# Modulation vectors of a two-layer backbone: direct products on TensorE replaced by wider sums on VectorE

## The chip, the core and the metric

The kernel runs on one core of a Trainium2 chip. The metric is the device time of one execution in microseconds, as the median of several; smaller is better. The engines are PE (TensorE, the matrix engine), DVE (VectorE), ACT (ScalarE), POOL (GpSimd) and SP, whose queue issues nearly all loads.

## The reference, cut to what matters

Two layers run over 256 latent and 256 context tokens of width 1024. Each layer is a feed-forward stage, a token mixer and a second feed-forward stage, and each of the three is wrapped in normalisations whose shift, scale and gate vectors come from the conditioning vectors `c` and `c_ctx` through one large matrix `w_ada` (1024 x 9216 for each layer, 36 MB in float32):

```python
def rms_norm(x, g):
    return x * rsqrt(mean(x * x, axis=-1) + EPS) * g
def ada_pre(x, mod, j, g):
    return rms_norm(x, g) * (1.0 + mod[..., 3 * j + 1, :]) + mod[..., 3 * j, :]
def ada_post(x, y, mod, j, g, w):
    return x + w * mod[..., 3 * j + 2, :] * rms_norm(y, g)
def macaron_ffn(x, mod, j, g_pre, g_post, w1, w3, w2):
    h = ada_pre(x, mod, j, g_pre)
    y = (silu(h @ w1) * (h @ w3)) @ w2
    return ada_post(x, y, mod, j, g_post, 0.5)
...
    mod_x = (silu(c) @ w_ada[l] + b_ada[l]).reshape(B, 1, 9, D)
    mod_c = (silu(c_ctx) @ w_ada[l] + b_ada[l]).reshape(1, 1, 9, D)
    # feed-forward (j=0), token mix (j=1), feed-forward (j=2), for latent and context tokens
```

## The kernel before, in words

The stages follow each other as F0_0 (first feed-forward of layer 0), mix0, F1_0, F0_1, mix1, F1_1. Activations lie transposed, 128 channels by tokens; the context tokens are columns 0 to 255, the latent ones 256 to 511. Each float32 weight tile is split into a high part (a cast on ACT, line 240, tile wh) and a low part (a subtraction on DVE, line 241, tile wl), and each product is made of three matrix products, lines 257 to 259 ("main products" below).

A feed-forward stage has 11 blocks gi, each with 256 columns of W1 and 256 of W3 (96 main products of 128x512). Behind each block stand the gates, lines 595 to 599: silu on ACT, a multiply on DVE (596), a cast, and a subtraction on DVE (599). Then come four groups dg of the down projection with W2; in dg 3 the two token streams are done one after the other by `part`. Weights are loaded by the SP queue into three raw tiles and split into four pairs wh, wl.

The modulation vectors are cut into units of 256 columns of `w_ada`, 36 a layer. The first eight of layer 0 are made in the setup. The other 64 are "fillers", and two ways are in use:

- Summed on DVE (`mod_acc`), 48 units: two in each of the blocks gi 0 to 7 of F0_0, F1_0 and F0_1, loaded by `preload` at the block before. A unit is 16 DVE operations of 128x256 (line 306 for the first of each column of `sc`, line 308 for the seven accumulations), which leave per-partition sums. Every fourth unit closes a batch: PE sums the partitions by products with ones (line 317), ACT copies the result (320), PE transposes it (four products, line 326), DVE adds the bias into `mods` (328).
- Direct products on PE (`mod_mm`), 16 units: eight are loaded at the end of F0_0 (the 8 in `FIN`) and eight at the end of mix0 (`MIXB`), and `flush`, called in `passes`, makes them at the start of mix0 and of F1_0. A unit is eight products with `sc` as the weights (line 277), an ACT copy (279), two small products (284) and a DVE add (285).

`passes` makes the first products of a stage, stream by stream. For the second stream the input still has to be normalised: `Post.steps` sums squares and cross terms (PE, lines 474 to 497; the row sums of line 488 come first), then runs a chain of small DVE operations (`rsqrt_cols`, lines 358 to 367) for the output norm of the stage that ends, a broadcast of its result over rows on PE (line 372), a second such chain for the input norm of the next stage, and a second broadcast. The multiplies of line 529 need the first broadcast, the scaled inputs of lines 387 (DVE), 395 (ACT) and 396 (DVE) the second. Line 348 makes gate vectors of the stage to come from `mods`.

PE, SP, DVE and ACT run in an order that a scheduler fixes when the program is built. It has no table by hand; the order follows from what each engine has to do and from `issue_after` for single instructions, so it can change where work is added or taken away.

Of the kernel before, what the change touches and what calls it, by code (L numbers as in the profile page):

```python
# [20 lines left out]
KD = 8  # L21
# [23 lines left out]
ACC, BX, MX = 3, 2, 3  # L45
FIN = ((16, 8), (16, 0), (16, 0), (0, 0))
MIXB = ((0, 8), (0, 0))
PU = 2

# [27 lines left out]
def body(tc, I, out, dbg=None):  # L77
    nc = tc.nc
    with tc.tile_pool(name="cst", bufs=1) as cst, \
# [188 lines left out]
        def settle():  # L268
            while late:
                late.pop(0)()  # L270
# [22 lines left out]
        batch = []  # L293

        def mod_acc(l, u, raw):
            if len(batch) % 2 == 0:
                pair = slab()
            else:
                pair = batch[-1][2]
            batch.append((l, u, pair))  # L300
            for s in range(2):
                t = pair[:, (len(batch) - 1) % 2, 256 * s:256 * s + 256]
                for k in range(KD):
                    w, c = raw[k // 4][:, k % 4, :], sc[:, k, s:s + 1]
                    if k == 0:
                        V.tensor_scalar(t, w, c, None, op0=ALU.mult)
                    else:
                        V.scalar_tensor_tensor(t, w, c, t, op0=ALU.mult, op1=ALU.add)  # L308
            if len(batch) < 4:
                return  # L310
            items = batch[:]
            batch.clear()

            def sums():
                bank = mx()
                for j in range(4):
                    mm(bank[32 * j:32 * j + 32, :], one1.to_broadcast([128, 32]), items[j][2][:, j % 2, :], start=True, stop=True,
                       tile_position=(0, 32 * j))
                sb = tmp()
                S.copy(sb, bank)  # L320

                def rest():
                    p2 = mx((128, 2, 2, 128))
                    for s in range(2):
                        for i in range(2):
                            nc.tensor.transpose(p2[:, s, i, :], sb[:, 256 * s + 128 * i:256 * s + 128 * i + 128], ident)
                    for j, (l, u, _) in enumerate(items):
                        V.tensor_tensor(mods[l][:, 2 * u:2 * u + 2, :], p2[:, :, :, 32 * j].rearrange("p s i -> p i s"),
                                        par[f"b{l}"][:, 2 * u:2 * u + 2, None].to_broadcast([128, 2, 2]), op=ALU.add)

                late.append(rest)

            late.append(sums)
# [218 lines left out]

        def preload(n):
            for _ in range(n):
                if fillers:
                    m = fillers.pop(0)
                    ahead.append((*m, mod_load(*m, True)))

        def flush(n):
            settle()  # L560
            for _ in range(n):
                if ahead:
                    mod_mm(*ahead.pop(0), S.copy)

# [8 lines left out]
        def passes(accs, h, sts, hook=None):  # L573
            n = len(ahead)
            for s_, (lo, hi, _) in enumerate(sts):
                flush(-(-n // len(sts)))
                for i in range(KD):
                    for j, (ps, w, c0) in enumerate(accs):
                        if hook:
                            hook(i, j)  # L580
                        end = mm3(ps[:, lo:hi], w[i:i + 1], c0, h[i:i + 1], lo, hi, i == 0, i == KD - 1)
                    if s_ == 0 and pend and i in (1, 5):
                        pend[0].step(end)
                drain(end)

        def ffn(l, f, h, post, streams, pre, first=(None, None)):
# [3 lines left out]
            units, hook = first  # L590
            nxt = []

            def gate(p1, p3):
# [8 lines left out]
            for gi in range(KF // 2):  # L602
# [36 lines left out]
                if gi + 1 == KF // 2:  # L639
                    nxt.append(unit(W2[0:1024, 0:256], 8))  # L640
                for _ in range(len(late)):
                    late.pop(0)()
                while ahead:
                    mod_acc(*ahead.pop(0))
                if gi < 9:
                    preload(min(PU, FIN[2 * l + f][0] - PU * gi))
            st = [slab(), slab()]
# [7 lines left out]
            for dg in range(4):  # L655
# [11 lines left out]
                if dg < 3 or len(streams) == 1:  # L667
# [10 lines left out]
                    for c in range(2):  # L678
                        post.chunk(2 * dg + c, ps[c], streams)
                    if dg == 3:  # L680
                        assert pre is None
# [9 lines left out]
                else:  # L691
# [16 lines left out]
                    part(1, 0)  # L708
                    part(0, 1)
                    part(0, 2)  # L710
                    for c in range(2):
                        post.chunk(6 + c, pss[0][c], [streams[0]])
# [7 lines left out]
                    pend.append(Pending(post.steps(streams[1], pre)))  # L720
            preload(FIN[2 * l + f][1])

# [73 lines left out]
        def mix(l, h, post, need_c, pre):  # L796
# [488 lines left out]
            ws = []  # L1285
            preload(MIXB[l][0])
            for dg in range(4):
# [25 lines left out]
            if not need_c:  # L1313
                drain()
            preload(MIXB[l][1])

# [70 lines left out]
        first = ((u1, u3), hook)  # L1387
        fillers += [(0, u) for u in range(8, 36)]
        fillers += [(1, u) for u in range(36)]
        for l in range(DEPTH):  # L1390
# [24 lines left out]
```

## Time and profile before

| | us |
|---|---|
| median of 3 runs | 2465.45 |
| lowest, highest | 2462.8, 2466.14 |
| profiled execution | 2463.13 |
| its span in the trace | 2461.4 |
| PE busy in the span | 2396.5 (97%) |
| DVE busy | 1449.1 (59%) |
| ACT busy | 974.4 (40%) |

Busy time of PE is modelled from pipelined instructions and isn't PE at its peak. The span is 2.3 us shorter than the execution, since it begins with the first instruction and ends with the last. PEclk is the share of full speed that TensorE's clock was granted; 0.50 is the lower of its two levels. Times in rows count from the span's start.

### The profile page before, as it was taken

To read this page: it belongs to the slowest core of one execution; us is meant where nothing else is said; L and a number is where in the kernel's file an instruction comes from. 1 tells how busy PE (TensorE), PEld (TensorE's weight loads), DVE (VectorE), ACT (ScalarE), POOL (GpSimd) and SP (SyncE) were. 2 spreads that over 40 slices of the span, in tenths; PEclk is the share of its full clock that TensorE was granted. 3 is DMA by queue.
4 is the path that set the end of the run, shared out by engine and by line. 5 is a ranking of instruction groups with operands and counts; after the bars stand their busy time and mean duration, and the time that the engine had idled before them with its cause. 6 is when DMAs were issued, how large, how long until landed. Compare 5 with 4: busy or idle time off the path is not lost. (4 is left out here: it accounts for less than half of the span.)

```text
span 2461.4 us, 35549 instructions
## 1 busy us (share of the span) xinstructions
PE 2396.5 (97%) x14042; PEld 2022.3 (82%) x14042; DVE 1449.1 (59%) x2965; ACT 974.4 (40%) x1603; POOL 240.4 (10%) x233
## 2 busy tenths in 40 slices
PE   7999999999999999999999989999999999998998
PEld 6877788788787788877777888777788888898998
DVE  6787534455654643748865356884436657657554
ACT  3322333333643723433223323232424365755543
POOL 2000021100000111400001120000312000023000
PEclk9999999999999999999999999999999999998999
DMA  7665233411123032455542325562323124354664
GB/s 263 197 195 165 71 111 110 160 52 53 43 70 86 27 102 87 132 185 188 173 152 86 93 62 186 173 188 86 99 84 92 52 62 123 100 147 129 189 184 133
DMA packets 300042, 301.04 MB, mean 122 GB/s; under 512 B 11709, under 2 KB 298742, under 8 KB 299876
## 3 DMA queue, kind: packets, MB, share of 16 engines
q1 hardware_dynamic: 299216, 298.04, 39.3%
q8 instruction: 110, 1.80, 0.3%
q0 software_dynamic: 512, 0.68, 0.2%
q14 instruction: 56, 0.46, 0.1%
q10 hardware_dynamic: 148, 0.06, 0.0%
HBM read 297.70 MB, written 1.05 MB: 121 GB/s over the span
## 5 line engine op out<-in xcount | busy, mean ns | idle before, releaser
L257 PE MATMUL a<-s,wh 128*128 128x512 f32 (+1 forms) x3266 | 1144.8, 351 | 13.6 <-ACT s L395 13.4
L258 PE MATMUL a<-s,wh 128*128 128x512 f32 (+1 forms) x3266 | 1143.1, 350 | 1.6 <-DVE s L396 1.2
L259 PE MATMUL a<-s,wl 128*128 128x512 f32 (+1 forms) x3266 | 1142.5, 350 | 0.0
L241 DVE TENSOR_TENSOR wl<-raw,wh 128x1024 fp32r<-128x1024 f32 (+1 forms) x414 | 523.0, 1270 | 510.0 <-ACT wh L240 507.6
L257 PEld LDWEIGHTS a<-s,wh 128*128 128x128 f32 x3266 | 619.4, 190 | 115.9 <-ACT s L395 14.4
L258 PEld LDWEIGHTS a<-s,wh 128*128 128x128 f32 x3266 | 620.8, 190 | 93.1 <-issue 8.2
L259 PEld LDWEIGHTS a<-s,wl 128*128 128x128 f32 x3266 | 620.8, 190 | 85.9 <-issue 3.4
L240 ACT CAST wh<-raw 128x1024 fp32r<-128x1024 f32 (+1 forms) x418 | 431.0, 1034 | 575.4 <-PE a L258 493.6
L308 DVE SCALAR_TENSOR_TENSOR s<-s,sc,s 128x256 f32<-128x256 f32 x672 | 273.2, 478 | 0.0
L413 POOL TENSOR_TENSOR s<-s,t 128x512 f32<-128x512 f32 (+1 forms) x35 | 55.2, 1576 | 1031.9 <-ACT s L409 1029.6
L598 ACT CAST s<-u 128x512 fp32r<-128x512 f32 (+1 forms) x88 | 49.5, 566 | 159.0 <-DVE u L596 141.2
L595 ACT ACTIVATE u<-a 128x512 f32<-128x512 f32 (+1 forms) x88 | 47.5, 542 | 158.2 <-PE a L259 158.2
L596 DVE TENSOR_TENSOR u<-u,a 128x512 f32<-128x512 f32 (+1 forms) x84 | 52.0, 619 | 73.7 <-PE a L259 72.7
L739 PE MATMUL a<-wh,s 128*128 128x256 f32 x256 | 72.8, 284 | 2.1 <-ACT s L742 1.6
L740 PE MATMUL a<-wl,s 128*128 128x256 f32 x256 | 73.0, 285 | 0.3 <-DVE wl L241 0.3
L741 PE MATMUL a<-wh,s 128*128 128x256 f32 x256 | 72.6, 284 | 0.0
L530 POOL TENSOR_TENSOR XT<-XT,s 128x256 f32<-128x256 f32 x72 | 55.0, 796 | 173.7 <-DVE s L529 159.6
L395 ACT ACTIVATE s<-t,mod 128x256 fp32r<-128x256 f32 x88 | 40.4, 502 | 77.9 <-DVE t L387 77.7
L1141 POOL TENSOR_TENSOR s<-s,u 128x512 f32<-128x512 f32 (+1 forms) x32 | 35.8, 1121 | 318.0 <-DVE u L1140 317.5
L599 DVE TENSOR_TENSOR s<-u,s 128x512 fp32r<-128x512 f32 (+1 forms) x88 | 53.9, 621 | 20.8 <-ACT s L598 20.6
L459 POOL TENSOR_TENSOR s<-s,u 128x512 f32<-128x512 f32 (+1 forms) x29 | 36.9, 1272 | 200.4 <-DVE u L455 199.7
L444 ACT ACTIVATE s<-a,R 128x256 f32<-128x256 f32 x77 | 34.0, 470 | 53.2 <-PE a L259 48.9
(340 smaller groups left out, 2417.1 us busy)
## 6 DMA issues: line engine op xcount, KB each, us to landing
raw<-in_ffn_w_dram SPq DMA_DIRECT2D x256, 512.0 KB, 3.8
s<-in_w_ada_dram SPq DMA_DIRECT2D x144, 512.0 KB, 6.8
raw<-in_w_in_dram SPq DMA_DIRECT2D x112, 512.0 KB, 3.7
raw<-in_w_out_dram SPq DMA_DIRECT2D x16, 512.0 KB, 3.4
raw<-in_ffn_w_dram SPq DMA_DIRECT2D x16, 256.0 KB, 2.6
raw<-in_w_branch_hg_dram SPq DMA_DIRECT2D x8, 512.0 KB, 3.9
raw<-in_w_branch_ml_dram SPq DMA_DIRECT2D x8, 512.0 KB, 3.4
raw<-in_w_branch_att_dram SPq DMA_DIRECT2D x8, 512.0 KB, 4.5
```

What stands on the lines that cost most here:

```text
L240: S.copy(hi[:, :n], raw[:, :n])
L241: (eng or V).tensor_tensor(lo[:, :n], raw[:, :n], hi[:, :n].bitcast(F32), op=ALU.subtract)
L257: mm(ps, hi, h[i][:, 0, a:b], start=first and i == 0, stop=False)
L258: mm(ps, hi, h[i][:, 1, a:b], start=False, stop=False)
L259: end = mm(ps, lo, h[i][:, 0, a:b], start=False, stop=last and i == n - 1)
L308: V.scalar_tensor_tensor(t, w, c, t, op0=ALU.mult, op1=ALU.add)
L413: eng.tensor_tensor(dst[:, a:b], dst[:, a:b], q[:, a:b], op=ALU.add)
L530: post_x.append(G.tensor_tensor(xt, xt, yt, op=ALU.add).ins)
L599: V.tensor_tensor(gt[:, 1, a:b], t[:, a:b], gt[:, 0, a:b].bitcast(F32), op=ALU.subtract)
L739: mm(ps, h[k][:, 0, tk], hi, start=k == 0, stop=False)
L740: mm(ps, h[k][:, 0, tk], lo, start=False, stop=False)
L741: mm(ps, h[k][:, 1, tk], hi, start=False, stop=k == KD - 1)
```

## The change

All 64 fillers are made on DVE, as 32 wide units of 512 columns. A wide unit is loaded in four pieces of 256 rows (`wide_load`, line 295, each 512 columns wide) and is 16 DVE operations of 128x512 (lines 309 and 311). A batch is now two wide units, with the same four ones-products (320), the copy (323), four transposes (328) and two adds (330). `FIN` lists for each feed-forward stage how many wide units are loaded at gi 0 to 7 (1, 1, 1, 2, 1, 1, 1, 1) and how many more for the down projection (three in F0_0, one each in F1_0 and F0_1); of the latter only the first half is loaded ahead, the second inside `mod_acc`. `mod_mm` remains for the first eight units in the setup; `flush` and `MIXB` are gone, so the starts of mix0 and F1_0 have no direct products, and no modulation weights are loaded between stages.

```diff
-FIN = ((16, 8), (16, 0), (16, 0), (0, 0))
-MIXB = ((0, 8), (0, 0))
-PU = 2
+FIN = (((1, 1, 1, 2, 1, 1, 1, 1), (1, 1, 1)), ((1, 1, 1, 2, 1, 1, 1, 1), (1,)), ((1, 1, 1, 2, 1, 1, 1, 1), (1,)), ((), ()))
...
+        def wide_load(l, u, i):
+            t = slab()
+            nc.sync.dma_start(t, I["w_ada"][l, 256 * i:256 * i + 256, 512 * u:512 * u + 512].rearrange("(k p) c -> p k c", p=128))
+            return t
...
+            t = slab()
+            batch.append((l, u, t))
+            for i in range(4):
+                r = raw[i] if i < len(raw) else wide_load(l, u, i)
+                for k in (2 * i, 2 * i + 1):
+                    for s in range(2):
+                        w, c = r[:, k % 2, :], sc[:, k, s:s + 1]
+                        if k == 0:
+                            V.tensor_scalar(t[:, s], w, c, None, op0=ALU.mult)
+                        else:
+                            V.scalar_tensor_tensor(t[:, s], w, c, t[:, s], op0=ALU.mult, op1=ALU.add)
+            if len(batch) < 2:
                 return
...
-        def flush(n):
-            settle()
-            for _ in range(n):
-                if ahead:
-                    mod_mm(*ahead.pop(0), S.copy)
+        def gather():
+            for _ in range(len(late)):
+                late.pop(0)()
+            while ahead:
+                mod_acc(*ahead.pop(0))
...
         def passes(accs, h, sts, hook=None):
-            n = len(ahead)
+            settle()
             for s_, (lo, hi, _) in enumerate(sts):
-                flush(-(-n // len(sts)))
...
+                gather()
+                if gi < len(now):
+                    preload(now[gi])
+            assert not ahead
+            preload(sum(then[:1]), 2)
...
                     for c in range(2):
                         post.chunk(2 * dg + c, ps[c], streams)
+                    gather()
+                    preload(sum(then[dg + 1:dg + 2]), 2)
...
                     part(0, 1)
+                    gather()
                     part(0, 2)
+                    settle()
...
-        fillers += [(0, u) for u in range(8, 36)]
-        fillers += [(1, u) for u in range(36)]
+        fillers += [(0, u) for u in range(4, 18)]
+        fillers += [(1, u) for u in range(18)]
```

Line numbers move by two from line 295 on: main products are lines 255 to 257 after, the split 239, the gates 596 to 600, the broadcast 374, the chain 360 to 369, line 529 is 531, 387 is 389.

The order of instructions changes at three places. In the order's rows a tile's letter says what it is: a, b, x are PSUM banks, s slabs, m small columns, wh and wl weights, t and u scratch.

First, PE in the start of mix0, second stream. Before:

```order
L284 MATMUL x_3553<-cf,t_3562 128x2 x2
L277 MATMUL x_3567<-s_3470,sc 32x256 x4
L277 MATMUL x_3567<-s_3472,sc 32x256 x4
L284 MATMUL x_3567<-cf,t_3576 128x2 x2
L277 MATMUL x_3581<-s_3474,sc 32x256 x4
L372 MATMUL x_3619<-cf,m_3437 128x128 x2
L372 MATMUL x_3683<-cf,m_3622 128x128 x2
L277 MATMUL x_3581<-s_3476,sc 32x256 x4
L284 MATMUL x_3581<-cf,t_3590 128x2 x2
L277 MATMUL x_3758<-s_3478,sc 32x256 x4
L257 MATMUL a_3535<-s_3367,wh_3513 128x256
```

After:

```order
L256 MATMUL a_3497<-s_3408,wh_3491 128x256
L257 MATMUL a_3497<-s_3408,wl_3492 128x256
L255 MATMUL b_3498<-s_3408,wh_3491 128x256
L256 MATMUL b_3498<-s_3408,wh_3491 128x256
L257 MATMUL b_3498<-s_3408,wl_3492 128x256
L374 MATMUL x_3587<-cf,m_3526 128x128 x2
L255 MATMUL a_3495<-s_3359,wh_3473 128x256
L255 MATMUL a_3496<-s_3359,wh_3473 128x256
L255 MATMUL a_3497<-s_3359,wh_3485 128x256
L255 MATMUL b_3498<-s_3359,wh_3485 128x256
L256 MATMUL a_3495<-s_3359,wh_3473 128x256
```

Before, the direct products (277, 284) stand among the main products and around the two broadcasts (372), which come in a row; after, only main products are there, and 20 of them part the first broadcast (374, 21 rows above the one shown) from the second.

Second, DVE at the same place, the second chain (from line 359, after 361). Before:

```order
L361 TENSOR_TENSOR m_3623<-m_3622 128x2
L362 TENSOR_TENSOR m_3623<-m_3623,m_3453 128x2
L363 SCALAR_TENSOR_TENSOR m_3624<-m_3623 128x2
L285 TENSOR_TENSOR mod_88<-x_3539,pb_146 128x4
L364 SCALAR_TENSOR_TENSOR m_3622<-m_3624,m_3622 128x2
L365 TENSOR_TENSOR m_3623<-m_3622 128x2
L366 TENSOR_TENSOR m_3623<-m_3623,m_3625 128x2
L367 SCALAR_TENSOR_TENSOR m_3622<-m_3623,m_3622 128x2
L285 TENSOR_TENSOR mod_88<-x_3553,pb_146 128x4
L285 TENSOR_TENSOR mod_88<-x_3567,pb_146 128x4
L529 TENSOR_TENSOR s_2565<-s_2565,x_3619 128x256 x2
```

After:

```order
L363 TENSOR_TENSOR m_3527<-m_3526 128x2
L531 TENSOR_TENSOR s_2672<-s_2672,x_3523 128x256
L364 TENSOR_TENSOR m_3527<-m_3527,m_3445 128x2
L531 TENSOR_TENSOR s_2899<-s_2899,x_3523 128x256
L365 SCALAR_TENSOR_TENSOR m_3528<-m_3527 128x2
L531 TENSOR_TENSOR s_2899<-s_2899,x_3523 128x256
L366 SCALAR_TENSOR_TENSOR m_3526<-m_3528,m_3526 128x2
L531 TENSOR_TENSOR s_3196<-s_3196,x_3523 128x256
L367 TENSOR_TENSOR m_3527<-m_3526 128x2
L531 TENSOR_TENSOR s_3196<-s_3196,x_3523 128x256
L368 TENSOR_TENSOR m_3527<-m_3527,m_3529 128x2
L369 SCALAR_TENSOR_TENSOR m_3526<-m_3527,m_3526 128x2
```

Before, the chain's steps stand together and the multiplies of line 529 (on slabs s, with the broadcast x) behind it; after, a multiply (531) stands between each two steps of the chain, and the line that closes it (369) comes last. The rows of F0_1 before alternate in the same way, with line 348 ahead of the last step.

Third, DVE in F0_0 where the fourth entry of `FIN`, 2, is summed (gi 4). At the same block before:

```order
L599 TENSOR_TENSOR s_1292<-u_1289,s_1292 128x512
L328 TENSOR_TENSOR mod_88<-x_1319,pb_146 128x4 x2
L306 TENSOR_SCALAR s_1328<-s_1175,sc 128x256 x2
L308 SCALAR_TENSOR_TENSOR s_1328<-s_1175,sc,s_1328 128x256 x6
L308 SCALAR_TENSOR_TENSOR s_1328<-s_1177,sc,s_1328 128x256 x8
L306 TENSOR_SCALAR s_1328<-s_1179,sc 128x256 x2
L308 SCALAR_TENSOR_TENSOR s_1328<-s_1179,sc,s_1328 128x256 x6
L308 SCALAR_TENSOR_TENSOR s_1328<-s_1181,sc,s_1328 128x256 x8
L241 TENSOR_TENSOR wl_1484<-raw_1481,wh_1483 128x1024
L241 TENSOR_TENSOR wl_1490<-raw_1487,wh_1489 128x1024
L596 TENSOR_TENSOR u_1469<-u_1469,a_1419 128x512
L348 SCALAR_TENSOR_TENSOR m_2402<-mod_88,ppost 128x16
```

After:

```order
L600 TENSOR_TENSOR s_1252<-u_1249,s_1252 128x512
L309 TENSOR_SCALAR s_1286<-s_1127,sc 128x512 x2
L311 SCALAR_TENSOR_TENSOR s_1286<-s_1127,sc,s_1286 128x512 x2
L311 SCALAR_TENSOR_TENSOR s_1286<-s_1129,sc,s_1286 128x512 x4
L311 SCALAR_TENSOR_TENSOR s_1286<-s_1131,sc,s_1286 128x512 x4
L311 SCALAR_TENSOR_TENSOR s_1286<-s_1133,sc,s_1286 128x512 x4
L309 TENSOR_SCALAR s_1303<-s_1135,sc 128x512 x2
L311 SCALAR_TENSOR_TENSOR s_1303<-s_1135,sc,s_1303 128x512 x2
L311 SCALAR_TENSOR_TENSOR s_1303<-s_1137,sc,s_1303 128x512 x4
L311 SCALAR_TENSOR_TENSOR s_1303<-s_1139,sc,s_1303 128x512 x4
L311 SCALAR_TENSOR_TENSOR s_1303<-s_1141,sc,s_1303 128x512 x4
L597 TENSOR_TENSOR u_1428<-u_1428,a_1378 128x512
```

Before, 32 operations of 128x256 stand between the gate's last subtraction (599) and the next splits (241); after, 32 of 128x512, and behind them two gate multiplies (597, the first of them is the last row shown) ahead of the first split.

## Rows read from the trace of the kernel before

**Rows 1.** First lines of the page: busy time, GB/s by slice, chain by line

```profile
PE 2396.5 (97%) x14042; PEld 2022.3 (82%) x14042; DVE 1449.1 (59%) x2965; ACT 974.4 (40%) x1603; POOL 240.4 (10%) x233
...
GB/s 263 197 195 165 71 111 110 160 52 53 43 70 86 27 102 87 132 185 188 173 152 86 93 62 186 173 188 86 99 84 92 52 62 123 100 147 129 189 184 133
...
PE a L258 5%; PE a L259 5%; PE a L257 5%; PE a L740 1%; PE a L739 1%; PE a L741 1%; PE x L1268 0%; PE x L851 0%; PE x L1090 0%; PE b L1208 0%; ACT wh L240 0%; DVE wl L241 0%; ACT L1118 0%; ACT s L1229 0%; PE x L1080 0%
```

**Rows 2.** Timeline of PE at three hand-overs (start us, us, engine, line, op, tiles)

```profile
413.13 0.64 PE L488 MATMUL x<-s,ones 128*32 128x256 f32 x8
...
1442.05 0.64 PE L488 MATMUL x<-s,ones 128*32 128x256 f32 x8
...
1841.14 0.64 PE L488 MATMUL x<-s,ones 128*32 128x256 f32 x8
```

**Rows 3.** Timeline of ACT: first read of the new stage's finished bank

```profile
467.99 0.60 ACT L811 ACTIVATE s<-a 128x512 f32<-128x512 f32 x1 [1.88 <-PE a L259]
...
1485.74 1.09 ACT L595 ACTIVATE u<-a 128x512 f32<-128x512 f32 x2 [3.46 <-PE a L259]
...
1879.74 0.60 ACT L811 ACTIVATE s<-a 128x512 f32<-128x512 f32 x1 [1.71 <-PE a L259]
```

**Rows 4.** Timeline of PE at F0_1's start; in brackets idle before and its releaser

```profile
1470.70 0.68 PE L372 MATMUL x<-cf,m 128*128 128x128 f32 x4 [3.94 <-DVE m L367]
1472.58 1.01 PE L257 MATMUL a<-s,wh 128*128 128x256 f32 x3 [1.20 <-ACT s L395]
```

**Rows 5.** Stretch of F0_1's start: length, busy by engine, PEclk, DMA share, GB/s

```profile
1471.50:1478.30 6.80, 5.72 (x27) 5.72 (x28) 6.48 (x16) 3.53 (x8) 0.00 (x0) 0.50 0.00 0
```

**Rows 6.** Timeline of DVE: second chain at F0_1, then at mix1

```profile
1469.03 0.41 DVE L529 TENSOR_TENSOR s<-s,x 128x256 f32<-128x256 f32 x1
...
1469.71 0.77 DVE L348 SCALAR_TENSOR_TENSOR m<-mod,ppost 128x16 f32<-128x16 f32 x1
1470.40 0.15 DVE L367 SCALAR_TENSOR_TENSOR m<-m,m 128x2 f32<-128x2 f32 x1
...
1865.21 0.16 DVE L367 SCALAR_TENSOR_TENSOR m<-m,m 128x2 f32<-128x2 f32 x1
```

**Rows 7.** Timeline of PE in F0_0: a run of sums, a set of transposes

```profile
125.46 0.40 PE L259 MATMUL a<-s,wl 128*128 128x512 f32 x1
125.79 1.06 PE L317 MATMUL x<-s,ones 128*32 128x512 f32 x8
...
127.12 0.39 PE L258 MATMUL a<-s,wh 128*128 128x512 f32 x1
127.36 0.40 PE L259 MATMUL a<-s,wl 128*128 128x512 f32 x1
...
148.97 0.39 PE L259 MATMUL a<-s,wl 128*128 128x512 f32 x1
149.21 0.60 PE L326 MATMUL x<-cf,t 128*128 128x128 f32 x4
...
149.88 0.39 PE L258 MATMUL a<-s,wh 128*128 128x512 f32 x1
```

**Rows 8.** Timeline of DVE in F0_0: a unit's accumulations, two weight splits

```profile
158.78 5.63 DVE L308 SCALAR_TENSOR_TENSOR s<-s,sc,s 128x256 f32<-128x256 f32 x14
...
186.28 1.22 DVE L241 TENSOR_TENSOR wl<-raw,wh 128x1024 fp32r<-128x1024 f32 x1
...
299.83 1.22 DVE L241 TENSOR_TENSOR wl<-raw,wh 128x1024 fp32r<-128x1024 f32 x1
```

**Rows 9.** Groups by shape: xcount, busy us in all, mean ns of one

```profile
L308 DVE SCALAR_TENSOR_TENSOR s<-s,sc,s 128x256 f32<-128x256 f32 x672 | 273.2, 478 | 0.0
...
L1075 DVE SCALAR_TENSOR_TENSOR s<-s,m 128x384 f32<-128x384 f32 x16 | 9.1, 614 | 0.0
```

**Rows 10.** Timeline of PE: first use of the two splits of rows 8

```profile
196.35 0.40 PE L259 MATMUL a<-s,wl 128*128 128x512 f32 x1
...
302.38 0.39 PE L259 MATMUL a<-s,wl 128*128 128x512 f32 x1
```

More of the change, by code (lines that the diff above doesn't have):

```diff
@@ L293, in body @@
         batch = []
+        def wide_load(l, u, i):
+            t = slab()
+            nc.sync.dma_start(t, I["w_ada"][l, 256 * i:256 * i + 256, 512 * u:512 * u + 512].rearrange("(k p) c -> p k c", p=128))
+            return t
         def mod_acc(l, u, raw):
[L296 to L309, printed above, removed]
+            t = slab()
[10 more added lines that the diff above has]
+            if len(batch) < 2:
                 return
@@ L316, in sums @@
                 for j in range(4):
-                    mm(bank[32 * j:32 * j + 32, :], one1.to_broadcast([128, 32]), items[j][2][:, j % 2, :], start=True, stop=True,
+                    mm(bank[32 * j:32 * j + 32, :], one1.to_broadcast([128, 32]), items[j // 2][2][:, j % 2, :], start=True, stop=True,
                        tile_position=(0, 32 * j))
@@ L322, in rest @@
                 def rest():
[L323 to L326, printed above, removed]
+                    p2 = mx((128, 4, 128))
+                    for i in range(4):
+                        nc.tensor.transpose(p2[:, i, :], sb[:, 128 * i:128 * i + 128], ident)
                     for j, (l, u, _) in enumerate(items):
-                        V.tensor_tensor(mods[l][:, 2 * u:2 * u + 2, :], p2[:, :, :, 32 * j].rearrange("p s i -> p i s"),
-                                        par[f"b{l}"][:, 2 * u:2 * u + 2, None].to_broadcast([128, 2, 2]), op=ALU.add)
+                        V.tensor_tensor(mods[l][:, 4 * u:4 * u + 4, :], cap(p2, 0, 128, 64 * j, [[128, 4], [32, 2]]),
+                                        par[f"b{l}"][:, 4 * u:4 * u + 4, None].to_broadcast([128, 4, 2]), op=ALU.add)
                 late.append(rest)
@@ L551, in body, with preload @@
         ahead = []
-        def preload(n):
+        def preload(n, parts=4):
             for _ in range(n):
-                if fillers:
-                    m = fillers.pop(0)
-                    ahead.append((*m, mod_load(*m, True)))
-        def flush(n):
-            settle()
-            for _ in range(n):
-                if ahead:
-                    mod_mm(*ahead.pop(0), S.copy)
+                m = fillers.pop(0)
+                ahead.append((*m, [wide_load(*m, i) for i in range(parts)]))
+        def gather():
[3 more added lines that the diff above has]
+                mod_acc(*ahead.pop(0))
         pend = []
@@ L591, in ffn @@
             nxt = []
+            now, then = FIN[2 * l + f]
             def gate(p1, p3):
@@ L640, in ffn @@
                     nxt.append(unit(W2[0:1024, 0:256], 8))
[L641 to L646, printed above, removed]
+                gather()
[3 more added lines that the diff above has]
+            preload(sum(then[:1]), 2)
             st = [slab(), slab()]
@@ L720, in ffn @@
                     pend.append(Pending(post.steps(streams[1], pre)))
-            preload(FIN[2 * l + f][1])
         def proj(Win, col0, n, h, a, b, cb):
@@ L1285, in mix @@
             ws = []
-            preload(MIXB[l][0])
             for dg in range(4):
@@ L1314, in mix @@
                 drain()
-            preload(MIXB[l][1])
         mark("setup")
```

## The prediction

> **What bounds the kernel now.** I read the page first. TensorE is busy for 97% of the span, VectorE (DVE) for 59%, and the chain of work that ended last runs through the main products of lines 257 to 259 [rows 1]. So the end is set by what stands in TensorE's queue and by its stops; DVE work costs time only where TensorE waits for it. Next I read the places where one stage hands over to the next and two short normalisation chains run on DVE. From the row sums at line 488 to the first read of the new stage's finished bank there are 413.13 to 467.99 = 54.86 us at the start of mix0, 1485.74 - 1442.05 = 43.69 at F0_1 and 1879.74 - 1841.14 = 38.60 at mix1 [rows 2, 3]. The first holds eight direct products, the others none. The starts of mix0 and mix1 are otherwise the same work, so eight units cost 54.86 - 38.60 = 16.26 us, or **2.03 us a unit**. (F1_0, which holds the other eight, starts with more products done ahead of line 488 and isn't compared with these.)
>
> Then I asked why F0_1, without direct products, takes 5.1 us longer than mix1. TensorE stops there for 3.94 us ahead of the second row broadcast (line 372) and for 1.20 us behind it [rows 4], and for the following 6.8 us its granted clock is 0.50, the lower of its two levels, 1.2 GHz [rows 5]. DVE's rows show why: at F0_1 the second chain's last step (line 367) comes at 1470.40, because each of its small steps stands behind a 0.41 us multiply of line 529 and one line-348 step; at mix1 the chain is done at 1865.21 and the multiplies follow it [rows 6].
>
> **The change part by part.**
>
> *Direct products leave.* At mix0's start eight units go, at most 8 x 2.03 = 16.3 us. But they also filled TensorE's time while DVE ran its chains, and the order moves with them: in the changed kernel DVE alternates multiplies and chain steps there, and TensorE has 20 products between the two broadcasts, both row for row as at F0_1 before (the order rows above show it). So I take F0_1's 43.69 us for this place and not mix1's 38.60, less the line-348 step, which the new order doesn't have there (1470.40 - 1469.71 = 0.7 us [rows 6]): 43.0. **Gain 11.9 us**; bounds 11.2 (43.69) and 16.3 (38.60).
>
> At F1_0's start another eight units go, again at most 16.3. There too the new order alternates, but TensorE has 36 products between the broadcasts instead of 20. A plain product of 512 columns takes 127.36 - 127.12 = 0.24 us [rows 7], one of 256 columns half of that. So F0_1's stop of 3.94 shrinks by 16 x 0.12 = 1.9 and by the 0.7 of line 348 to 1.3; the stop behind the broadcast stays near 1.0 (1.20 less two products). 16.3 - 2.3 = 14.0 at full clock. With a stretch at 0.50 as long as F0_1's it loses 6.8 x 0.5 = 3.4 more, 10.6. I take a value between the two, **12 us**; bounds 9 and 14.
>
> The rule that speaks against removing filler products is in the Trainium skill, "TensorE: Matmul & The Clock Gate", section "Why this matters for your kernels": gaps in TensorE's work put its clock back to the lower level, and a kernel should avoid them. This trace agrees at F0_1 (granted 0.50 behind the two stops [rows 4, 5]); by that rule F1_0 would gain its 10.6, and without it 14.0.
>
> *512 columns on DVE.* Before, a unit of 256 columns is 14 accumulations in 5.63 us, 0.40 each, at a mean duration of 478 ns; the nearest wider row is 614 ns at 384 columns [rows 8, 9]. That is 136 ns for 128 columns more, so 512 columns give an estimated 0.40 + 0.27 = 0.67 us. A wide unit (14 of these and two first steps, line 309, for which I take 0.4) is then some 10.1 us, against some 12.3 for two narrow ones (28 x 0.40 and four first steps at 0.3). In an ordinary block, where a wide unit takes the place of two narrow ones, DVE is 2 us earlier. It lies beside TensorE's 96 products, 23 us, and so neither gains nor costs.
>
> *The block with two wide units* (once in each of F0_0, F1_0, F0_1) has a DVE run of 20.2 us instead of 12.3. Behind it stand two gate multiplies (taken at 0.6 each) and the split of the next block's first weights. Before, that split ends at 186.28 + 1.22 = 187.50 [rows 8] and TensorE first uses it at 196.35 [rows 10], a margin of 8.85. 8.85 - 7.9 - 1.2 - 0.25 (two line-330 steps) is about -0.5, and TensorE is itself delayed by a run of sums there. So 0 to 1.7 us each; I take 0.5, **1.5 us in all**.
>
> *Down projection.* Five wide units now run there. At dg 0 before, the first split ends at 299.83 + 1.22 = 301.05 and is used at 302.38 [rows 8, 10]: 1.3 us of margin behind a 12.3 us run. A 10.1 us run comes there now, and another one stands between the post chunks of dg 0. I take 1 us for three stages (0 to 3). In F0_0's dg 3 the third unit loads its last rows only when slots come free behind part (1, 0), and its 10 us stand on DVE ahead of the last two weight splits; TensorE's run of sums waits for it too. Between 1 and 4 us; I take 2.
>
> *Sums.* A run of ones-products delays the main products by 127.12 - 125.46 - 0.47 = 1.19 us, a set of four transposes by 149.88 - 148.97 - 0.47 = 0.44 (0.47 is two plain steps) [rows 7]. 12 batches become 16. By the order TensorE has 18 runs of sums and 12 of transposes before, 20 and 20 now (some are cut in two by main products): 2 x 1.19 + 8 x 0.44 = 5.9, less about one for the pieces with a single transpose or two: **4.8 us** (4 to 7).
>
> *Nothing else on the path.* The loads carry the same 4 MB a block in 2 KB rows instead of 1 KB; the double block takes 6 MB in 23 us, about 260 GB/s, which the first slice of the page shows moved [rows 1]. Waits of the SP queue for a slab stand at the same kind of place as before, and the weights queued behind them have the margin of 8.85 us worked out above. The ScalarE copies are as wide as before.
>
> *Sum*: gains 11.9 + 12 = 23.9; costs 4.8 + 1.5 + 1 + 2 = 9.3; **net -14.6 us**. The profiled execution took 2463.1 us (span 2461.4), so it becomes 2448.5; it lies 2.3 us below the median of 2465.45, to which I apply the same difference: **2451 us**. With all gains low and all costs high: -(11.2 + 9) + (7 + 5 + 3 + 4) = -1; all the other way: -30.3 + 5 = -25. These ends together are unlikely; likeliest case alone 2441 to 2460.
>
> **The rivals.**
>
> *The whole TensorE time comes back.* If the stops at mix0 and F1_0 stay as small as at mix1, the net is 2 x 16.3 - 9.3 = 23 us, 2442, and less where the costs stay low. For it: mix1's start, the same work without direct products. Against it: the DVE order is F0_1's.
>
> *Filler was free.* The eight units only stood in time in which TensorE would have waited, at both places: gains of 11.2 and 9 against costs near their upper ends, net -1 to -5, within what a measurement tells (0.2% is 4.9 us). For it: 5.1 us lost at F0_1. Against it: even F0_1 in its present form is 11.2 us shorter than mix0.
>
> *Slower: the long DVE run starves TensorE.* Its place is the double block: behind 20.2 us of accumulation stand the gate multiplies that free PSUM banks, and all splits. If the wide accumulation costs twice the narrow one (0.79 us, no saving), the run is 24 us, 3.8 later; the first split is then some 4.3 us late in three stages, and at dg 0 and dg 3 of each stage 2 to 4 us more, each stop long enough for a stretch at 0.50 (another 1.7 to 3.4). That is 3 x (4.3 + 3.4) + 3 x 6 = 41, with the sums 46 against 24 of gain: +22, or 2487. It decides from a cost of 0.75 us an accumulation. Against it: the slope from 256 to 384 columns, 0.67.
>
> **How the numbers follow.** The forecast as worked out (2441 to 2460): 0.66. Whole time back (below 2441): 0.13. Filler free or costs at their upper ends (2460 to 2470): 0.13. Starved (above 2470): 0.08. The range that leaves out no more than 2 in 10 reaches down into the first rival and up into the second: 2438 to 2464. A measurement of this kernel can tell about 0.2% from no change, 2460.5 to 2470.4. Faster: 0.66 + 0.13 = 0.79; same 0.13; slower 0.08.
>
> **What would show it.** In the changed kernel's trace: from the row sums (now line 490) to the first read of the finished bank, 43 us at mix0 and 26 to 30 at F1_0; a stop ahead of the second broadcast (line 374) of 3 to 4 us at mix0 and 1 to 2 at F1_0, and stretches at 0.50 behind them; accumulations of 512 columns with starts 0.67 us apart; a stop of at most 1.7 us for a split behind the double block. The prediction is wrong if mix0's start takes 39 us (then the order of DVE isn't what makes F0_1 slow), or if TensorE waits for line 239 by more than 10 us in all.

## The result and the profile after

| | before | after |
|---|---|---|
| median, us (4 runs each) | 2464.25 | 2442.53 |
| lowest to highest | 2462.8 to 2466.14 | 2441.34 to 2444.2 |
| profiled execution | 2463.13 | 2444.2 |
| its span | 2461.4 | 2442.4 |

The ratio is 0.9909 with a 95% interval of 0.9896 to 0.9921: 21.7 us faster by the medians, 18.9 by the two profiled executions (the one after is the slowest of its four). The forecast was 14.6 faster, 2451, with a range of 2438 to 2464.

The page after, busy time (compare [rows 1]):

```profile
PE 2374.4 (97%) x13770; PEld 2012.4 (82%) x13770; DVE 1479.2 (61%) x2677; ACT 970.4 (40%) x1591; POOL 239.3 (10%) x233
```

TensorE's share of the span is the same 97%; 22 us of busy time are gone from it, and DVE is busy for 30 us more. To see where the 19 us of the two traces lie, I cut both at the row sums (line 488 before, 490 after), which stand at the same work in both. Timeline of PE after:

```profile
401.38 0.64 PE L490 MATMUL x<-s,ones 128*32 128x256 f32 x8
...
417.88 0.64 PE L490 MATMUL x<-s,ones 128*32 128x256 f32 x8
...
1039.67 0.64 PE L490 MATMUL x<-s,ones 128*32 128x256 f32 x8
...
1422.13 0.64 PE L490 MATMUL x<-s,ones 128*32 128x256 f32 x8
...
1822.24 0.64 PE L490 MATMUL x<-s,ones 128*32 128x256 f32 x8
```

The two of before that [rows 2] don't show:

```profile
400.15 0.64 PE L488 MATMUL x<-s,ones 128*32 128x256 f32 x8
...
1046.33 0.64 PE L488 MATMUL x<-s,ones 128*32 128x256 f32 x8
```

| stretch | before | after | change |
|---|---|---|---|
| F0_0 up to its dg 3 | 400.15 | 401.38 | +1.2 |
| dg 3 of F0_0 | 12.98 | 16.50 | +3.5 |
| mix0 | 633.20 | 621.79 | -11.4 |
| F1_0 | 395.72 | 382.46 | -13.3 |
| F0_1 | 399.09 | 400.11 | +1.0 |
| mix1, F1_1 | 620.26 | 620.16 | -0.1 |

The gain is in the two stretches that had direct products. The first row alone counts from the span's start and so holds the start-up: the first silu of the gates comes at 56.73 after and at 56.00 before, which is 0.7 of the 1.2 us. ACT's first read of the finished bank, after, at mix0 and F1_0 (compare [rows 3]):

```profile
460.86 0.60 ACT L814 ACTIVATE s<-a 128x512 f32<-128x512 f32 x1 [2.16 <-PE a L257]
...
1066.03 1.09 ACT L596 ACTIVATE u<-a 128x512 f32<-128x512 f32 x2 [2.16 <-PE a L257]
```

and before, at F1_0:

```profile
1086.81 1.09 ACT L595 ACTIVATE u<-a 128x512 f32<-128x512 f32 x2 [3.38 <-PE a L259]
```

So mix0's start takes 460.86 - 417.88 = 42.98 us instead of 54.86 (-11.9), and F1_0's 1066.03 - 1039.67 = 26.36 instead of 1086.81 - 1046.33 = 40.48 (-14.1). These two are 26.0 us; 7 us are given back elsewhere, half of it in dg 3.

TensorE's stops at these starts after (start, length, idle before in brackets; compare [rows 4]; the first three rows are mix0, the last F1_0):

```profile
426.44 0.50 PE L255 MATMUL a<-s,wh 128*128 128x256 f32 x2 [2.09 <-ACT s L397]
...
446.34 1.20 PE L374 MATMUL x<-cf,m 128*128 128x128 f32 x4 [3.86 <-DVE m L369]
448.73 0.58 PE L255 MATMUL a<-s,wh 128*128 128x256 f32 x1 [1.19 <-ACT s L397]
...
1053.24 0.68 PE L374 MATMUL x<-cf,m 128*128 128x128 f32 x4 [1.99 <-DVE m L369]
```

The granted clock behind them, the last column but two (compare [rows 5]); the third row lies behind F1_0's stop:

```profile
428.00:431.50 3.50, 3.50 (x19) 3.50 (x18) 3.50 (x10) 2.10 (x6) 0.00 (x0) 0.53 0.15 54
447.50:452.00 4.50, 3.31 (x16) 3.27 (x16) 4.35 (x12) 2.61 (x6) 0.00 (x0) 0.50 0.00 0
1053.50:1057.00 3.50, 3.50 (x31) 3.47 (x31) 2.96 (x8) 1.39 (x4) 0.00 (x0) 1.00 0.00 0
```

At mix0 the stop of 3.86 us has come that F0_1 had before, with a stretch at 0.50 behind it. At F1_0 the stop is 1.99 us, and the clock stays at 1.00. Last, TensorE's longest waits for DVE and ACT after:

```profile
PE x L374 <- DVE m L369: 19.7, 9, 5.4
PE a L255 <- ACT s L397: 13.8, 7, 3.3
```

No wait of 0.4 us or more is for a weight split (line 239).

### The profile page after: what moved, and what is told of

Its sections match the earlier page's. It is cut to its first block, busy times and chain, and to the rows that moved or that the text cites. A ratio compares the mean times of both kernels' runs of the same rounds, so it can differ in the third digit from the quotient of the medians.

```text
span 2442.4 us, 34697 instructions
## 1 busy us (share of the span) xinstructions
PE 2374.4 (97%) x13770; PEld 2012.4 (82%) x13770; DVE 1479.2 (61%) x2677; ACT 970.4 (40%) x1591; POOL 239.3 (10%) x233
## 5 line engine op out<-in xcount | busy, mean ns | idle before, releaser
L255 PE MATMUL a<-s,wh 128*128 128x512 f32 (+1 forms) x3266 | 1145.2, 352 | 14.1 <-ACT s L397 13.8
L239 DVE TENSOR_TENSOR wl<-raw,wh 128x1024 fp32r<-128x1024 f32 (+1 forms) x414 | 515.7, 1255 | 469.2 <-ACT wh L238 466.7
L311 DVE SCALAR_TENSOR_TENSOR s<-s,sc,s 128x512 f32<-128x512 f32 x448 | 306.9, 763 | 0.0
```

The costliest lines, as they stand in the source:

```text
L239: (eng or V).tensor_tensor(lo[:, :n], raw[:, :n], hi[:, :n].bitcast(F32), op=ALU.subtract)
L255: mm(ps, hi, h[i][:, 0, a:b], start=first and i == 0, stop=False)
L311: V.scalar_tensor_tensor(t[:, s], w, c, t[:, s], op0=ALU.mult, op1=ALU.add)
```

## The experiments

The reading after the result, theory A: the change gains TensorE's time for the direct products, less the stops that DVE's alternating order makes at the two starts; the width of the DVE operations only makes room. Rivals are named with each run. All ratios below are to the kernel before.

### The direct products left out of the kernel before (e_none)

```diff
-FIN = ((16, 8), (16, 0), (16, 0), (0, 0))
-MIXB = ((0, 8), (0, 0))
+FIN = ((16, 0), (16, 0), (16, 0), (0, 0))
+MIXB = ((0, 0), (0, 0))
...
-        fillers += [(0, u) for u in range(8, 36)]
-        fillers += [(1, u) for u in range(36)]
+        fillers += [(0, u) for u in range(8, 24)]
+        fillers += [(1, u) for u in range(4, 36)]
```

> The kernel before without its 16 units of direct products, and nothing else: their loads, products, copies and adds are left out, and their part of the modulation vectors stays zero. DVE still sums 48 units of 256 columns. Theory A (the gain of the change is TensorE's time for the direct products, less the stops that its new order makes at the two starts): mix0's start takes 43 us and F1_0's 26.4, as in the changed kernel, so 11.9 + 14.1 = 26 us less than before, about 2438 (2436 to 2441); the changed kernel gives some 5 us of that back for its added sums. Rival B (the wider DVE operations and longer load rows bring most of the gain): well under half of the changed kernel's 21.7 us, 2454 or more.

Measured: 2437.97 us, ratio 0.9896 (0.9879 to 0.9912), 27.0 less than before on that chip. PE's row sums and ACT's first reads at mix0 and F1_0:

```profile
412.44 0.64 PE L490 MATMUL x<-s,ones 128*32 128x256 f32 x8
...
1032.38 0.64 PE L490 MATMUL x<-s,ones 128*32 128x256 f32 x8
```

```profile
453.55 0.60 ACT L813 ACTIVATE s<-a 128x512 f32<-128x512 f32 x1 [2.16 <-PE a L261]
...
1058.94 1.09 ACT L597 ACTIVATE u<-a 128x512 f32<-128x512 f32 x2 [2.22 <-PE a L261]
```

41.1 us at mix0 and 26.6 at F1_0. F1_0 is as expected; mix0 is 1.9 below the expected 43. The stop ahead of the broadcast is the same (3.85 us), but the granted clock over this start is 0.96, against 0.88 in the changed kernel. Removing the products alone, with all sums still 256 columns wide, brings more than the whole gain of the change. Rival B, that the wider operations bring it, falls. The loads of the 16 units are gone here too, but they weren't what held TensorE up: in the trace of before its waits at mix0's start are for ACT and DVE alone, and at F1_0's it has none.

### The width taken back (e_narrow)

```diff
-                    for s in range(2):
-                        w, c = r[:, k % 2, :], sc[:, k, s:s + 1]
+                    for s, h in ((0, 0), (1, 0), (0, 256), (1, 256)):
+                        w, c, o = r[:, k % 2, h:h + 256], sc[:, k, s:s + 1], t[:, s, h:h + 256]
                         if k == 0:
-                            V.tensor_scalar(t[:, s], w, c, None, op0=ALU.mult)
+                            V.tensor_scalar(o, w, c, None, op0=ALU.mult)
                         else:
-                            V.scalar_tensor_tensor(t[:, s], w, c, t[:, s], op0=ALU.mult, op1=ALU.add)
+                            V.scalar_tensor_tensor(o, w, c, o, op0=ALU.mult, op1=ALU.add)
```

> The changed kernel with one size changed back: each operation of 512 columns in the sums on DVE is made as two of 256; loads, batches and places are the same. Theory A: DVE's run is 12.3 us a unit instead of 10.1 and 24.6 in the double block; in the ordinary blocks this is hidden, in the double block the margin of 1.4 us turns into a wait of about 3, and at dg 1 a margin near zero turns into 2, in three stages: 3 x 5 = 15 at most, 2446 to 2458, likeliest 2452. Rival B: the whole gain goes, 2460 to 2464. Rival D (DVE has room everywhere, the width is of no account): 2442 to 2444.

Measured: 2460.78 us, ratio 0.9988 (0.9976 to 1.0001), from 2454.64 to 2469.31 in ten runs. That is within rival B's numbers and above theory A's range: a miss for A in size. The trace (its execution took 2457.54) shows the mechanism A named, only dearer. DVE in F0_0's double block, the two runs of accumulations and the split behind them, and PE's run of sums there:

```profile
152.52 11.17 DVE L311 SCALAR_TENSOR_TENSOR s<-s,sc,s 128x256 f32<-128x256 f32 x28
...
164.66 11.16 DVE L311 SCALAR_TENSOR_TENSOR s<-s,sc,s 128x256 f32<-128x256 f32 x28
...
176.94 1.21 DVE L239 TENSOR_TENSOR wl<-raw,wh 128x1024 fp32r<-128x1024 f32 x1
```

```profile
175.57 2.22 PE L320 MATMUL x<-s,ones 128*32 128x512 f32 x4 [1.62 <-DVE s L311]
```

DVE's runs are 12.1 us for a unit, and the split that ended at 175.34 in the changed kernel (below) ends at 178.15. TensorE's waits:

```profile
PE a L257 <- DVE wl L239: 5.2, 5, 1.7
PE x L320 <- DVE s L311: 4.8, 3, 1.7
```

The sums stand in TensorE's queue ahead of the main products, so TensorE stops first for the accumulations (three times up to 1.7 us) and then at dg 1 for the split. By the cuts of the table above, F0_0 up to dg 3 takes 4.2 us more than in the changed kernel, F1_0 4.6 and F0_1 3.6. So e_none has the gain without the width, but with all 64 units on DVE at these places nearly all of it is lost without the width. Over the ten executions the time goes with the mean granted clock of each, from 2454.64 us at 0.986 to 2469.31 at 0.979. The profiled one has 0.985, those near the median 0.983 or 0.984; so the 3 us between the two go with the clock.

### The chain first (e_chain), and the same order in the kernel before (e_bchain)

```diff
-                    with tc.issue_after(tail[0]) if self.mk[0] == DEPTH - 1 and st is self.streams[-1] else nullcontext():
+                    with tc.issue_after(tail[0]) if st is self.streams[-1] else nullcontext():
```

> The changed kernel with one order changed: the multiplies of line 531 for the last stream wait for the end of the second chain in every stage, which the kernel does in layer 1 only. Theory A (F0_1's, and now mix0's and F1_0's, stop ahead of the second broadcast comes from DVE's alternating order): mix0's start falls from 43.0 to 38.6 us, F0_1's from 43.7 to about 38.6, F1_0's by its stop of 2 us to 24.5, the stretches at half the clock behind them go, so 11 us less than the changed kernel, about 2431 (2429 to 2435). Rival C (the multiplies then start late, POOL's additions and the scaled inputs come late in their turn, and the stop only moves behind the broadcast): within 3 us of the changed kernel, 2439 to 2444.

Measured: 2429.51 us, ratio 0.9857 (0.9843 to 0.9872): 13 us less than the changed kernel, and **faster than both**. DVE at mix0's start, the last step of the chain and the multiplies behind it:

```profile
438.53 0.16 DVE L369 SCALAR_TENSOR_TENSOR m<-m,m 128x2 f32<-128x2 f32 x1
438.61 1.08 DVE L531 TENSOR_TENSOR s<-s,x 128x256 f32<-128x256 f32 x3
```

PE's row sums at the three starts and its stops at the first (PE's rows, then ACT's first reads):

```profile
416.17 0.64 PE L490 MATMUL x<-s,ones 128*32 128x256 f32 x8
...
438.84 0.68 PE L374 MATMUL x<-cf,m 128*128 128x128 f32 x4
...
440.95 0.62 PE L255 MATMUL a<-s,wh 128*128 128x256 f32 x3 [0.96 <-ACT s L397]
...
1031.90 0.64 PE L490 MATMUL x<-s,ones 128*32 128x256 f32 x8
...
1411.93 0.64 PE L490 MATMUL x<-s,ones 128*32 128x256 f32 x8
```

```profile
453.05 0.60 ACT L814 ACTIVATE s<-a 128x512 f32<-128x512 f32 x1 [1.70 <-PE a L257]
...
1055.96 1.09 ACT L596 ACTIVATE u<-a 128x512 f32<-128x512 f32 x2 [1.11 <-PE a L257]
...
1449.24 1.09 ACT L596 ACTIVATE u<-a 128x512 f32<-128x512 f32 x2 [3.01 <-PE a L257]
```

36.9 us at mix0 instead of 43.0, 24.1 at F1_0 instead of 26.4, 37.3 at F0_1 instead of 1466.35 - 1422.13 = 44.2 (43.7 before). The stop ahead of the second broadcast (438.84) is gone, one of 0.96 is left behind it, and the clock stays at 1.00 through the whole of mix0's start:

```profile
416.17:453.05 36.88, 33.03 (x266) 31.05 (x266) 30.85 (x86) 15.53 (x28) 12.41 (x16) 1.00 0.23 65
```

F1_0's start has the clock at 1.00 in both traces, so its 2.3 us are the order's alone. Mix0's and F0_1's starts have two stretches at 0.50 each in the changed kernel (0.88 over the whole start), a shorter one behind the first stop, which is the same in both kernels, and a longer one at the stop for the second broadcast; e_chain has neither. What the first is worth shows at mix1's start, where both kernels have the same order and only the clock differs (the changed kernel, then e_chain):

```profile
1822.24:1860.71 38.47, 34.23 (x266) 32.46 (x266) 30.39 (x84) 15.54 (x28) 12.20 (x16) 0.96 0.22 63
...
1805.22:1842.50 37.28, 32.99 (x266) 31.00 (x266) 30.11 (x84) 15.55 (x27) 12.22 (x16) 1.00 0.23 64
```

That is 1.2 us. So of mix0's 6.1 us about 5 are the order's, with the stretch at 0.50 that came with its stop, and about 1.2 belong to the other stretch; for the same reason most of the 1.7 us by which 36.9 is below the expected 38.6 isn't the order's. The alternating order is what costs the time at these starts, and rival C falls. By the cuts mix0 is 6.1 us shorter than in the changed kernel, F1_0 2.4, F0_1 6.8 and the last stretch 1.3 (1.2 of it at mix1's start, as shown), 16.6 in all; the medians are 13 apart, since this profiled execution, 2425.89, is the lowest of its four and the changed kernel's the highest of its own.

> The kernel before, with its 16 units of direct products, and only the order of e_chain: the multiplies for the last stream behind the second chain. By the order this moves instructions at F0_1 alone; at mix0 and F1_0 the kernel before has the chain first already. Theory A (direct products and the alternating order are two separate costs, and the second was there before at F0_1): F0_1's start falls from 43.7 to 37.5 us as in e_chain, 6 us less than before, about 2458 (2456 to 2461). Then removing the direct products is worth about 29 us at equal order (2458 against e_chain's 2429.5). Rival C (the order only matters where direct products are gone): within 2 us of before.

Measured: 2458.02 us, ratio 0.9966 (0.9953 to 0.9979), 8.2 less than before on that chip. F0_1's start takes 1481.98 - 1443.11 = 38.9 us instead of 43.7, and its whole stretch is 5.0 us shorter. It is 1.4 above the expected 37.5: the stretch at 0.50 behind the first stop is still there (0.96 over the whole start), which e_chain doesn't have. The last stretch, in which this edit moves nothing, is 2.0 shorter, 1.3 of it at mix1's start (37.3 instead of 38.6), where the clock stays at 1.00. So 5 of the 8.2 us are shown to come from the order. The mean granted clock is 0.989 or 0.990 in all five executions and 0.984 to 0.987 in the 13 of the kernel before beside them; whether the order keeps the clock up at later places too isn't settled. The order was worth having before the change already, at F0_1. At equal order, removing the direct products and summing all units on DVE is worth 0.9857 / 0.9966, about 27 us by the medians, against 29 expected; in the changed kernel 21.7 are seen because its new order brings F0_1's stop to mix0 and a smaller one to F1_0.

### Where the units stand on DVE (e_dg3, e_nodual, e_chain_nodual)

```diff
# e_dg3
-FIN = (((1, 1, 1, 2, 1, 1, 1, 1), (1, 1, 1)), ...
+FIN = (((1, 2, 1, 2, 1, 1, 1, 1), (1, 1)), ...
# e_nodual and e_chain_nodual, the same in F1_0 and F0_1
-FIN = (((1, 1, 1, 2, 1, 1, 1, 1), (1, 1, 1)), ...
+FIN = (((1, 1, 1, 1, 1, 1, 1, 1, 1), (1, 1, 1)), ...
```

> The changed kernel with F0_0's third unit of the down projection moved into a second double block (gi 1 of F0_0 loads two). Theory A (the unit in dg 3 costs 3.5 us because its run of sums is cut in two in the middle of the single-stream products, and a unit elsewhere costs 1 to 1.6): 2 to 2.5 us less than the changed kernel, about 2440. If instead a double block has a cost of its own that the first one only hid (its margin was 1.4 us): no gain or a loss, 2442 to 2446.

Measured: 2449.32 us, ratio 0.9938 (0.9923 to 0.9953), 7 more than the changed kernel and above both ranges. Its dg 3 is 3.1 us shorter (13.4 instead of 16.5), as A said, but F0_0 ahead of it takes 408.7 instead of 401.4. So moving the unit of dg 3 into a second double block costs more than it saves. What the 7.3 us are is shown only in part: the last silu of the blocks comes 3.1 us later (283.19 instead of 280.05), and in the down projection TensorE stops once for a split, 1.59 us. The rest wasn't tried.

> The changed kernel without double blocks: nine blocks with one wide unit each (gi 0 to 8) in F0_0, F1_0 and F0_1. Theory A (the double block makes no wait for a split, but cuts a run of sums in two and delays it, 1.7 us in F0_0's trace): 1 to 1.5 us a stage less, 2439 (2437 to 2441). Rival E (the tenth DVE run stands closer to the down projection and its splits come late there, margins 2.6 us at dg 0 and none at dg 1): the same or up to 5 us more than the changed kernel, 2442 to 2448.

Measured: 2459.7 us, ratio 0.9978 (0.9967 to 0.999), 17 more than the changed kernel; rival E, and dearer than it said. DVE ahead of dg 0 in F0_0 (the ninth unit's accumulations and the first W2 split), and TensorE there:

```profile
294.63 9.36 DVE L311 SCALAR_TENSOR_TENSOR s<-s,sc,s 128x512 f32<-128x512 f32 x14
...
305.26 1.22 DVE L239 TENSOR_TENSOR wl<-raw,wh 128x1024 fp32r<-128x1024 f32 x1
```

```profile
303.48 1.61 PE L320 MATMUL x<-s,ones 128*32 128x512 f32 x4 [1.20 <-DVE s L311]
306.53 0.50 PE L257 MATMUL a<-s,wl 128*128 128x512 f32 x1 [1.44 <-DVE wl L239]
```

The ninth unit's run ends at 303.99, where the changed kernel has no sums. TensorE stops 1.20 us for it, makes the sums, and stops 1.44 for the split, in each of the three stages. F0_0 up to dg 3 is 4.9 us longer than in the changed kernel, F1_0 5.3, F0_1 3.9. The double block at gi 4 is what keeps the last blocks free.

> Both edits, the order of e_chain and no double blocks. Theory A: they act in different stretches and add up: e_chain's 2429.5 less 3, 2426 (2424 to 2429). Rival E: 2430 to 2436.

Measured: 2448.25 us, ratio 0.9928 (0.9913 to 0.9943): above both ranges, on rival E's side and, as in e_nodual, dearer than it said. Against e_nodual the chain order gives 11.5 us here, against 13 without that edit, so the two effects add up to within 1.5 us. Mix0's start, with e_chain's order and, unlike there, a stretch at 0.50 behind its first stop, takes 38.0 us:

```profile
424.86:462.90 38.04, 34.20 (x266) 32.43 (x266) 30.88 (x86) 15.54 (x28) 12.41 (x16) 0.96 0.23 63
```

Against e_chain's 36.9 that is the 1.2 us of mix1's start once more.

### The sums left out (e_nosums)

```diff
+        for m_ in mods:
+            V.memset(m_, 0.0)
...
-            late.append(sums)
+            if False:
+                late.append(sums)
```

> The changed kernel without what closes a batch: no ones-products, copies, transposes and adds; the DVE sums stay, and the modulation vectors they would give are zero. It prices the term of the prediction that four more batches make. Theory A (a batch costs TensorE 1.19 + 0.44 = 1.63 us when its runs are whole, and more where they are cut, as in dg 3 with 3.5): 16 batches cost 26 to 30, about 2414 (2411 to 2418). Rival F (part of it lies in time in which TensorE would wait for a split anyway): under 20, above 2422.

Measured: 2424.58 us, ratio 0.9825 (0.9804 to 0.9846): 18 us less than the changed kernel, 1.1 a batch, by its number rival F. By the cuts, F1_0 and F0_1, with five batches each, are 7.4 and 7.7 us shorter, 1.5 a batch, which is near A's price; dg 3 is 3.5 shorter. The 16 batches fall short of 26 because F0_0 ahead of dg 3 gains only 3.2 for five and mix0, with zero vectors, takes 1.6 longer. What makes up these two wasn't tried.

## Why the prediction was right, by its own steps

**Bound and price of the direct products: right.** TensorE set the end, and 2.03 us a unit gave 16.3 at each start. With the chain first and, as before, only the stretch at 0.50 behind the first stop, mix0's start is 54.86 - 38.04 = 16.8 us shorter (e_chain_nodual), 2.10 a unit. e_none gives 27.0 for both starts, less than twice that, since its stops are in it.

**mix0's start: the mechanism right, the 0.1 us luck.** Forecast 43.0, measured 42.98, because the order of DVE showed F0_1's start there. Here the mechanism was tested by e_chain: with the chain first it is 36.9. But in the six traces with the alternating order mix0's start takes from 41.1 us (e_none) to 44.1 (e_narrow). F0_1's start before, from which I took the number, and mix0's in the changed kernel's trace happen to have the same granted clock, 0.88 over the whole start. The rival "the whole TensorE time comes back" gave 2442, the number that came out, but not its reason: the stops were not small.

**F1_0's start: mis-sized by 2 us.** Forecast gain 12, measured 14.1. The stop ahead of the broadcast was 1.99 (forecast 1.3) and none over 0.3 us stood behind it (forecast 1.0). The larger part is the clock: I took half of a stretch at 0.50, which was 1.7 us, and the granted clock stayed at 1.00, here and in the five other traces with this order (26.4 to 26.6 us). The gaps that the Trainium skill ("TensorE: Matmul & The Clock Gate", "Why this matters for your kernels") tells a kernel to avoid are longer than F1_0's stop, so the 10.6 that I drew from it didn't follow. Behind mix0's first stop of 2.09 us, which is shorter than those too, the lower clock did come, and there the measurement decides.

**512 columns: right.** Forecast 0.67 us an accumulation; 14 take 9.37 us, 0.67 each, in this double block (DVE's rows: the first of the two units, the split behind both, and the first W2 split ahead of dg 0; then TensorE's rows):

```profile
153.57 9.37 DVE L311 SCALAR_TENSOR_TENSOR s<-s,sc,s 128x512 f32<-128x512 f32 x14
...
174.11 1.23 DVE L239 TENSOR_TENSOR wl<-raw,wh 128x1024 fp32r<-128x1024 f32 x1
...
298.08 1.22 DVE L239 TENSOR_TENSOR wl<-raw,wh 128x1024 fp32r<-128x1024 f32 x1
```

```profile
175.80 1.04 PE L320 MATMUL x<-s,ones 128*32 128x512 f32 x2
176.78 0.51 PE L257 MATMUL a<-s,wl 128*128 128x512 f32 x1
...
301.90 0.39 PE L257 MATMUL a<-s,wl 128*128 128x512 f32 x1
```

**Waits for splits: not there.** I had put 1.5 us on the double blocks, 1 on dg 0 and 2 on dg 3 as waits for DVE. In the double block the split ends at 174.11 + 1.23 = 175.34, and TensorE, which has just made a piece of a run of sums, first uses it at 176.78: a margin of 1.4, where I had worked out -0.5 and the sums beside it. dg 0's margin went from 1.3 to 2.6 (298.08 + 1.22 against 301.90). The step that failed for dg 3 is the mechanism: its 3.5 us are not a wait. PE's rows:

```profile
401.84 2.06 PE L320 MATMUL x<-s,ones 128*32 128x512 f32 x6
...
405.06 1.04 PE L320 MATMUL x<-s,ones 128*32 128x512 f32 x2
...
406.85 0.54 PE L328 MATMUL x<-cf,t 128*128 128x128 f32 x3
```

The run of sums is cut in two there by single-stream products, and its pieces take 2.06 and 1.04 us where a whole run takes 1.06 [rows 7]; with the transposes that is 3.6. In e_nosums, without them, dg 3 takes 13.0 again, as before. The term I gave to DVE (2) is a cost of TensorE's own; with the batch's 1.63 among my sums I had 3.6 for dg 3, so its size came out by luck. Why the first piece, which follows the row sums of line 490, takes as long as 2.06 wasn't tried.

**Sums: about right.** Costs beyond the starts are 26.0 - 19.0 = 7.0 by the two traces, against 9.3 forecast. With dg 3's 3.5 set apart, 3.5 are left for the three other new batches. The price of a batch can't be read from them, since 0.7 of start-up and 0.5 of F0_1's start (44.2 instead of 43.7) are in it; e_nosums gives 1.5 in F1_0 and F0_1, near the 1.63 of a whole batch in [rows 7].

**The slower rival: its mechanism is real, its price was too high.** e_narrow is its condition, 512 columns at twice the narrow cost (2 x 11.17 / 28 = 0.80 us): TensorE did stop for the sums and the splits in all three stages, and the gain went, but to 2460.8 and not to the 2487 I had worked out.

**Sum.** 26.0 - 7.0 = 19.0 instead of 14.6: 2.1 from F1_0, 2.3 from costs that came out lower. The other 2.7 us to the medians' 21.7 are scatter between runs of one kernel: the profiled execution before lies 1.1 us below its median, the one after 1.7 above.

## What to carry to other kernels

Before work is taken off the engine that bounds, ask what else happened in its time: here it covered two chains of small operations, and 5 of the 17 us that mix0's start had to give at a like clock came back only when the order of the engine that runs the chain was put right. Read the new order at the places that lose work; a place elsewhere in the same trace that already has that order gives its time, here within 2 us (43.0 against 41.1 to 44.1). And where an engine off the path takes more work, the width of its operations and the block they stand in decide whether the bound one waits: here two runs in a block with margin made TensorE wait for nothing, and one run in the block ahead of the tight splits cost 4 to 5 us a stage.

## What wasn't expected

A stop's length doesn't tell what the clock does. Behind mix0's first stop of 2.09 us in the changed kernel the granted clock is 0.53 from 428.0 to 431.5; behind F1_0's of 1.99 it stays at 1.00. And in e_chain the same stop of 2.09 at the same place leaves it at 1.00, as the row of mix0's whole start in its section shows. PE's row of that stop:

```profile
424.73 0.50 PE L255 MATMUL a<-s,wh 128*128 128x256 f32 x2 [2.09 <-ACT s L397]
```

At mix1's start all ten traces have the same stop of 2.5 us; in six a stretch at 0.50 follows and the start takes 38.5 to 38.8 us, in four the clock stays at 1.00 and the start takes 37.3. So an edit that is worth 1 or 2 us at one place can't be read from a single trace without the clock beside it.

The start-up differs between executions by more than most edits here. The first main product of the changed kernel's profiled execution and of e_chain's:

```profile
24.08 0.79 PE L255 MATMUL a<-s,wh 128*128 128x512 f32 x1 [3.35 <-ACT s L397]
```

```profile
21.20 0.80 PE L255 MATMUL a<-s,wh 128*128 128x512 f32 x1 [1.91 <-ACT s L397]
```

2.9 us apart, and still 1.7 at F0_0's dg 3 (401.4 against 399.7). The waits ahead of it are for the first loads and the first scaled inputs. The earlier one is the lowest of its kernel's four executions, the later one the highest. So a difference of 2 us between two single traces says little if it counts from the span's start, as those of F0_0 ahead of dg 3 do here; from one row sum to the next the start-up drops out.
